# One inference step of a hybrid HGRN2 / RWKV-7 / short-conv layer: the RWKV stage laid out in 137 slots of TensorE's order

## The chip, the core and the metric

The kernel runs on one core of a Trainium2 chip. The metric is the device time of one execution in microseconds (us). The engines are named as in the profile: PE is TensorE's matmul, PEld its weight load, DVE VectorE, ACT ScalarE, POOL GpSimd, SP SyncE, which issues the DMAs. A kernel line is written L135.

## What is computed

One layer of a recurrent decoder takes 256 new tokens of one sequence and 8 tokens for each of 8 sampled sequences, 320 token columns in all. The layer's input is normalised and multiplied by one wide matrix; three branches (HGRN2, RWKV-7, a short convolution) work on its parts, are multiplied back to the model's width, gated and merged; an output matrix and a squared-ReLU MLP follow. The part that matters here is the RWKV branch:

```python
h = _rmsnorm(x, g_pre_mix)
proj = jnp.einsum('btd,de->bte', h, w_in)
rw = proj[..., OFF_RW:OFF_SC]
prev = jnp.concatenate([rw_prev[:, None], rw[:, :-1]], axis=1)
xs = rw + (prev - rw) * rw_mu
r, kr, vr, wd, ad, gd = jnp.split(xs, cuts, axis=-1)
w_log = -jax.nn.softplus(-(rw_w0 + jnp.tanh(wd) @ rw_w2)) - 0.5
decay = jnp.exp(-jnp.exp(w_log))
a = jax.nn.sigmoid(rw_a0 + ad @ rw_a2)
g = jax.nn.sigmoid(gd) @ rw_g2
kk = hs(kr * rw_k_k)
kk = kk / jnp.maximum(jnp.sqrt(jnp.sum(kk * kk, -1, keepdims=True)), 1e-12)
k = kr * (1.0 + (a - 1.0) * rw_k_a)
# per token and head:
#   S = S (diag(w) - kk^T (a*kk)) + v^T k ;  o = S r
o_rw, rw_S = _rwkv7_scan(r_, w_, k_, v_, kk, a_, rw_S0)
# group norm of o_rw per head, plus a bonus (sum of r*k*rw_r_k) * v, times g
y_b = o_rw @ w_pb
```

The model's width is 2048, the RWKV branch has 16 heads of width 64. The kernel evaluates the scan in chunks of 64 tokens, each with a triangular inverse.

## The kernel before

**Dense work.** Every large product is done in three matmuls of float32r halves, hi times ah, hi times al, lo times ah (L135 to L137 in `dense`), 128x320 each. `granule` loads 128x1024 weights (`raw`), and `split` makes `whi_t` on ScalarE (L109) and `wlo_t` on VectorE (L110), each in two pieces of 512. One output tile of the projection takes two granules, 16 k-steps and 48 matmuls. The order of the stages is: input norm and first tiles, RWKV stage (with the short convolution's tiles in it), HGRN with the merge of w_pc, the merges of w_pb and w_pa, output matrix, MLP.

**The RWKV stage** goes over 8 pairs of heads j (called heads here, j from 0), with two heads of 64 in the 128 partitions. For each there is
- `shift_mix`, three times: a projected tile (k, r, v) is taken out of PSUM into R (L305, L306), POOL makes the difference to the token before (L311), VectorE mixes (L314, L316).
- `rwkv_front`: the two small products for decay and a (L389), their activations (L395 to L397), the running product of decays Wp (L401), W (L403), its reciprocal Wi (L405); then the norm of kk: the square (L409), its sum over each head by a 128x320 matmul with a matrix of ones (L411), and one over its root in `rsqrt`, that is ScalarE's root (L170), VectorE's reciprocal (L171), two products on POOL and two VectorE passes (L174, L175); the normalised kk (L415) goes into LYR and BK, and transposes of v and BK follow (L440, L460). L451 sums r*k for the bonus.
- `rwkv_solve`: products of LYR and BK (L486), masked into Nb and GB (L495 to L500); the inverse of the 16x16 diagonal blocks on VectorE, 15 products and 15 sums (L517, L519) on a tile of 40 partitions that is reached through DRAM; then the inverse is widened to 32 and 64 with small matmuls (L542, L546, L552), whose results go back by L543, L549, L553.
- `rwkv_chunks`: for each of 4 chunks three steps, one behind the other: L586 with L587, copied to Y by ScalarE (L589); L594, copied to X by VectorE (L596); L598 with L599, which gives the next state (L604, L606). Then the sample part (L615 to L639) and the group norm (L649 to L668), whose matmul is L678, and at last L683.

What comes of it is B (L684), and the convolution's is Cb; both stay in SBUF until `merge_split` splits them for the merges.

**What sets the order.** The program is traced head by head; a list scheduler with simulated times then orders each engine's instructions by priority, the earlier traced first. Each engine runs its own list in order and waits on semaphores. On TensorE the small matmuls of a chain so come to stand between dense ones.

Of the kernel before, what the change touches and what calls it, by code (L numbers as in the profile page):

```python
# [88 lines left out]
SC_ORDER = ((), (0,), (1,), (2,), (3,), (4,), (5,), (6, 7))  # L89


class K:
# [31 lines left out]

    def dense(self, granules, ah, al):
# [53 lines left out]
    def build(self):  # L179
# [94 lines left out]
        self.merge_split(self.Cb)  # L274
# [5 lines left out]
        for src, i, w in ((self.B, 1, io["w_pb"]), (self.A, 0, io["w_pa"])):  # L280
            self.merge_split(src)
# [14 lines left out]
    def shift_mix(self, wp, n, name, packed):  # L296

        nc = self.nc
        ps = self.proj(n)
        i = n - RR  # L300
        R = wp.tile([128, 329], F32, name="R" + name, bufs=1)
        Rs = R[:, 257:329].rearrange("p (b w) -> p b w", w=9)
        nc.gpsimd.tensor_copy(R[:, 0:1], self.zero)
        nc.gpsimd.tensor_copy(Rs[:, :, 0], self.prev[:, i, :])
        nc.vector.tensor_mul(R[:, 1:257], ps[:, :NP], self.rs[:, :NP])  # L305
        nc.vector.tensor_mul(Rs[:, :, 1:9], ps[:, NP:].rearrange("p (b w) -> p b w", w=8),  # L306
                             self.rs[:, NP:].rearrange("p (b w) -> p b w", w=8))
# [12 lines left out]
    def rwkv(self, cx):  # L320
# [21 lines left out]
        for nm, cols in (("Nb", 640), ("GB0", 640), ("GB1", 640), ("LX", 256), ("Ms", 256), ("Od", 640)):  # L342
# [9 lines left out]
        for d in self.dP:  # L352
            nc.sync.dma_start(d[0:128 * 640].rearrange("(p x) -> p x", x=640), Z["Nb"])
        self.Z = Z
        xwa = self.shift_mix(w2, RWA, "k", True)
        self.L = kp.tile([128, NT], F32, name="L")
        nc.scalar.activation(self.L[0:64, :], xwa[0:64, :], AF.Tanh)
        nc.scalar.copy(self.L[64:128, :], xwa[64:128, :])
        self.Lg = kp.tile([128, NT], F32, name="Lg")
        st = [self.rwkv_front(0, wp, w2)]  # L360
        self.rwkv_solve(0, st[0], wp)
        xg = self.shift_mix(w2, RG, "v", True)
        nc.scalar.activation(self.Lg, xg, AF.Sigmoid)
        st.append(self.rwkv_front(1, wp, w2))
        for j in range(8):
            if j < 7:
                self.rwkv_solve(j + 1, st[j + 1], wp)
            self.rwkv_chunks(j, st[j], wp, w2)
            for i in SC_ORDER[j]:
                self.short_conv(i)  # L370
            if j < 6:
                st.append(self.rwkv_front(j + 2, wp, w2))
        nc.sync.dma_start(io["o_cv"], self.cvo)
        nc.sync.dma_start(io["o_shift"], self.shl)

    def rwkv_front(self, j, wp, w2):
# [25 lines left out]
        W = w2.tile([128, NT], F32, name="W")  # L402
        V.tensor_mul(W, Wp, wt[:, 1:])  # L403
        Wi = wp.tile([128, NT], F32, name="Wi")
        V.reciprocal(Wi, W)  # L405


        sq = wp.tile([128, NT], F32, name="sq")
        S.activation(sq, kx, AF.Square, scale=self.par("kk", j))  # L409
        ss = self.pa.tile([128, 512], F32, name="pa_t")  # L410
        T.matmul(ss[:, :NT], self.cst("bo1"), sq, start=True, stop=True)  # L411
        V.tensor_scalar_max(sq, ss[:, :NT], 1e-24)
        rn = self.rsqrt(wp, sq, "rn")
        kkn = rn
        V.scalar_tensor_tensor(kkn, kx, self.par("kk", j), rn, ALU.mult, ALU.mult)  # L415

        LYR = w2.tile([128, 5, 4, 64], F32, name="LYR")
        BK = w2.tile([128, 5, 3, 64], F32, name="BK")
# [12 lines left out]
        S.copy(BK[:, :, 2, :], BK[:, :, 0, :])  # L431
        rk = wp.tile([128, NT], F32, name="rkk")
        V.scalar_tensor_tensor(rk, r, self.par("rk", j), t, ALU.mult, ALU.mult)


        X = w2.tile([128, 5, 2, 64], F32, name="X")
# [12 lines left out]

        bs = self.pa.tile([128, 512], F32, name="pa_t")  # L450
# [12 lines left out]

        return W, LYR, BK, X, BT, vx

    def rwkv_solve(self, j, front, wp):
        nc, io = self.nc, self.io
        V, G, S, T = nc.vector, nc.gpsimd, nc.scalar, nc.tensor
        W, LYR, BK, X, BT, vx = front
# [5 lines left out]
        Nb = Z["Nb"].rearrange("p (c w) -> p c w", w=128)  # L475
        GB = Z["GB%d" % (j % 2)].rearrange("p (c h w) -> p c h w", h=2, w=64)
        for mk, cc in (("mkp", slice(0, 4)), ("mks", slice(4, 5))):
# [10 lines left out]
            for h, rows in ((0, lo), (1, hi)):  # L488
# [19 lines left out]
        nc.sync.dma_start(flat(dN), Z["Nb"])  # L508
        Nd = wp.tile([40, 16, 16], F32, name="Nd")
        Pd = wp.tile([40, 16, 16], F32, name="Pd")  # L510
        for c in range(5):
            nc.sync.dma_start(Nd[8 * c:8 * c + 8], blocks(dN, c))
        S.copy(Pd.rearrange("p s t -> p (s t)"), self.cst("eye16")[0:40])
        for u in range(15, 0, -1):
            w = 16 - u
            t1 = wp.tile([40, 16, 16], F32, name="t1")
            V.tensor_mul(t1[:, 0:u, 0:w], Nd[:, 0:u, u:u + 1].to_broadcast([40, u, w]),  # L517
                         Pd[:, u:u + 1, u:16].to_broadcast([40, u, w]))
            V.tensor_add(Pd[:, 0:u, u:16], Pd[:, 0:u, u:16], t1[:, 0:u, 0:w])  # L519
# [18 lines left out]
        for h in (16, 32):  # L538
            T3 = Z["T%d" % h].rearrange("p (c w) -> p c w", w=128)
# [687 lines left out]
```

## Time and profile before

| | |
|---|---|
| median of 3 runs | 2457.81 us (2457.61 to 2459.03) |
| the profiled execution | 2458.85 us |
| its span in the profile | 2457.0 us |
| mean granted TensorE clock | 0.993 |
| TensorE busy, whole span | 98% |
| VectorE, ScalarE, POOL busy | 61%, 41%, 15% |
| TensorE busy in the RWKV stage, 45 to 606 us | 540.57 of 561 us |
| HGRN with w_pc, 606 to 1000 us (start of it) | 394.00 of 394 us |

The page is of one execution on the chip. Busy time of matmuls is modelled at its end, as they are pipelined, so a busy TensorE need not be at its full pace; its pace is read from the number of matmuls in a stretch. The waits are the idle time of an engine and the instruction that ended it. The granted clock of TensorE is 1 where it runs at full speed.

### The profile page before, as it was taken

To read this page: it belongs to the slowest core of one execution; us is meant where nothing else is said; L and a number is where in the kernel's file an instruction comes from. 1 tells how busy PE (TensorE), PEld (TensorE's weight loads), DVE (VectorE), ACT (ScalarE), POOL (GpSimd) and SP (SyncE) were. 2 spreads that over 40 slices of the span, in tenths; PEclk is the share of its full clock that TensorE was granted. 3 is DMA by queue.
4 is the path that set the end of the run, shared out by engine and by line. 5 is a ranking of instruction groups with operands and counts; after the bars stand their busy time and mean duration, and the time that the engine had idled before them with its cause. 6 is when DMAs were issued, how large, how long until landed. Compare 5 with 4: busy or idle time off the path is not lost.

```text
span 2457.0 us, 41891 instructions
## 1 busy us (share of the span) xinstructions
PE 2413.6 (98%) x16134; PEld 2317.3 (94%) x16134; DVE 1508.5 (61%) x3209; ACT 1017.5 (41%) x2049; POOL 358.8 (15%) x508
## 2 busy tenths in 40 slices
PE   8999999999999999999999999999999999999998
PEld 7888898889999999999999897999999999999997
DVE  6788888876666666655555436654555555555555
ACT  6444444434444444433443335334333333333333
POOL 4323332221001100011111331200000000000003
PEclk9999999999999999999999999999999999999999
DMA  5423333334433443344444654444444444444443
GB/s 194 132 90 122 108 116 115 119 121 149 141 132 136 143 141 131 129 154 150 146 155 148 233 180 161 155 149 152 148 153 147 153 148 153 148 149 152 149 152 129
DMA packets 132278, 355.05 MB, mean 145 GB/s; under 512 B 34928, under 2 KB 43504, under 8 KB 132080
## 3 DMA queue, kind: packets, MB, share of 16 engines
q1 hardware_dynamic: 132080, 352.38, 41.8%
q8 instruction: 128, 2.10, 0.3%
q14 instruction: 70, 0.57, 0.1%
HBM read 337.19 MB, written 15.14 MB: 143 GB/s over the span
## 4 chain that ended last, share of the span: by engine, by line
PE 90%; DVE 7%; POOL 1%; ACT 1%; issue 1%; DMA 1%; SPq 0%; DVEq 0%; ACTq 0%; POOLq 0%
PE mm_t L135 26%; PE mm_t L137 26%; PE mm_t L136 26%; DVE wlo_t L110 1%; PE pi L486 1%; PE plv_t L851 1%; PE pho_t L901 1%; PE pi L546 1%; DVE t L517 0%; PE pi L552 0%; PE wide_t L972 0%; PE py_t L586 0%; PE wide_t L973 0%; DVE Wi L405 0%; DVE rn_y L171 0%
## 5 line engine op out<-in xcount | busy, mean ns | idle before, releaser
L109 ACT CAST whi_t<-raw 128x512 fp32r<-128x512 f32 x1192 | 687.3, 618 | 1103.0 <-PE mm_t L136 757.2
L110 DVE TENSOR_TENSOR wlo_t<-raw,whi_t 128x512 fp32r<-128x512 f32 x1192 | 829.1, 724 | 309.3 <-ACT whi_t L109 299.6
L135 PE MATMUL mm_t<-xh,whi_t 128*128 128x320 f32 x2048 | 645.2, 315 | 1.7 <-DVE Rk L306 1.2
L137 PE MATMUL mm_t<-xh,wlo_t 128*128 128x320 f32 x2048 | 641.2, 313 | 0.4 <-DVE wlo_t L110 0.4
L136 PE MATMUL mm_t<-xl,whi_t 128*128 128x320 f32 x2048 | 640.3, 313 | 0.0
L135 PEld LDWEIGHTS mm_t<-xh,whi_t 128*128 128x128 f32 x2048 | 386.2, 189 | 6.7 <-issue 1.8
L137 PEld LDWEIGHTS mm_t<-xh,wlo_t 128*128 128x128 f32 x2048 | 386.0, 189 | 3.0 <-issue 0.9
L136 PEld LDWEIGHTS mm_t<-xl,whi_t 128*128 128x128 f32 x2048 | 386.1, 189 | 1.6 <-issue 0.2
L135 PE MATMUL mm_t<-hh,whi_t 128*128 128x320 f32 x1232 | 381.6, 310 | 0.0
L136 PE MATMUL mm_t<-hl,whi_t 128*128 128x320 f32 x1232 | 380.9, 309 | 0.0
L137 PE MATMUL mm_t<-hh,wlo_t 128*128 128x320 f32 x1232 | 380.8, 309 | 0.0
L137 PE MATMUL mm_t<-rh,wlo_t 128*128 128x320 f32 x1024 | 316.4, 309 | 0.0
L135 PE MATMUL mm_t<-rh,whi_t 128*128 128x320 f32 x1024 | 316.4, 309 | 0.0
L136 PE MATMUL mm_t<-rl,whi_t 128*128 128x320 f32 x1024 | 316.4, 309 | 0.0
L135 PEld LDWEIGHTS mm_t<-hh,whi_t 128*128 128x128 f32 x1232 | 231.7, 188 | 6.5 <-ACT sqt L1058 4.9
L136 PEld LDWEIGHTS mm_t<-hl,whi_t 128*128 128x128 f32 x1232 | 231.6, 188 | 0.0
L137 PEld LDWEIGHTS mm_t<-hh,wlo_t 128*128 128x128 f32 x1232 | 231.6, 188 | 0.0
L136 PEld LDWEIGHTS mm_t<-rl,whi_t 128*128 128x128 f32 x1024 | 192.2, 188 | 0.0
L135 PEld LDWEIGHTS mm_t<-rh,whi_t 128*128 128x128 f32 x1024 | 192.2, 188 | 0.0
L137 PEld LDWEIGHTS mm_t<-rh,wlo_t 128*128 128x128 f32 x1024 | 192.2, 188 | 0.0
L1129 DVE TENSOR_TENSOR m<-m,mm_t 128x320 f32<-128x320 f32 x112 | 54.6, 488 | 189.4 <-PE mm_t L137 189.4
L1059 POOL TENSOR_TENSOR ssf<-ssf,sqt 128x320 f32<-128x320 f32 x14 | 14.1, 1004 | 841.9 <-issue 809.6
(425 smaller groups left out, 2744.4 us busy)
## 6 DMA issues: line engine op xcount, KB each, us to landing
raw<-w_in SPq DMA_DIRECT2D x256, 512.0 KB
raw<-w_ff SPq DMA_DIRECT2D x256, 512.0 KB
raw<-w_o SPq DMA_DIRECT2D x32, 512.0 KB
hs<-s_hg SPq DMA_DIRECT2D x16, 512.0 KB
raw<-w_pc SPq DMA_DIRECT2D x16, 512.0 KB
raw<-w_pb SPq DMA_DIRECT2D x16, 512.0 KB
raw<-w_pa SPq DMA_DIRECT2D x16, 512.0 KB
o_hgs<-hsn SPq DMA_DIRECT2D x16, 256.0 KB
```

What stands on the lines that cost most here:

```text
L109: self.nc.scalar.copy(hi, src)
L110: self.nc.vector.tensor_sub(lo, src, hi)
L135: mmul(ps[:, :NT], hi[:, w], ah[:, i, :], start=(i == 0), stop=False)
L136: mmul(ps[:, :NT], hi[:, w], al[:, i, :], start=False, stop=False)
L137: mmul(ps[:, :NT], lo[:, w], ah[:, i, :], start=False, stop=(i == n - 1))
L486: T.matmul(pp[h][:, i, :], BK[rows, c, h:h + 2, :].rearrange("p a w -> p (a w)"), LYR[rows, c, h:4:2, :], start=True, stop=True)
L546: T.matmul(ps[:, half(i)], Nb[:, i, :], cols(Mm[:, i, :], h, 0), start=True, stop=True)
L851: T.matmul(ps[:, 0:128], KM, rh[:, 0:2 * hb], start=True, stop=True)
L901: T.matmul(op[:, 256:320], s0[:, b, :], QX[:, 64 * b:64 * b + 64], start=(b == 0), stop=False)
L1059: (nc.vector if last else nc.gpsimd).tensor_add(acc, acc, t)
L1129: nc.vector.tensor_add(d, d, ps)
```

## The change

1. TensorE's order in the RWKV stage is laid by hand. Every part of a head (front, solve, chunk, sample, tail) becomes a generator that yields between its steps, and so do the dense tiles. A table gives each step of head j a slot, counted from 12(j+1); there are 137 slots, and 768 dense k-steps are spread over them: 7 a slot in the first 12, about 5.5 a slot after that. Only TensorE's order is fixed so; the other engines' lists still come from the scheduler, with a higher priority for the chunk, sample and late solve steps and a still higher one for the copies of projected tiles out of PSUM.
2. A granule is split in one piece of 1024, and up to three granules are fetched ahead.
3. The norm of kk: three 128x2 matmuls (L491 of the new kernel) sum the squares with the tokens in the partitions, six tiny VectorE operations on 128x6 (L495 to L501) and ScalarE's root (L496) make one over the root, ScalarE spreads it to 128x384 (L503), and three transposes (L507 to L509) bring it back.
4. The 16x16 inverse: 4x4 blocks first, then products of blocks of 4 and of 8, 18 VectorE operations in all.
5. `shift_mix` takes a tile out of PSUM in one operation and mixes in one.
6. More buffers (Nb 2, GB 3, LYR, X, BT 3, W 4, xsv 4; BK 1). B and Cb go to DRAM (dB, dC) and are loaded back by `merge_split`.

The core of the diff:

```diff
-SC_ORDER = ((), (0,), (1,), (2,), (3,), (4,), (5,), (6, 7))
+NSLOT = 12
+URGENT = 1000
+FRONT = (-6, -5, -3, 0, 1, 2)
+SOLVE = (0, 2, 9, 15, 16, 17, 18, 19, 20)
+SAMPLE = (20, 21, 22, 23)
+CONV = (3, 0, 1, 1, 1, 1, 1, 0)
+CHUNK = tuple(range(21, 33))
+TAIL = (33, 39, 40)
...
-        for q in range(2):
-            c = slice(512 * q, 512 * q + 512)
+        for q in range(pieces):
+            c = slice(1024 // pieces * q, 1024 // pieces * (q + 1))
             self.split(hi[:, c], lo[:, c], raw[:, c])
...
-    def dense(self, granules, ah, al):
+    def dense_steps(self, granules, ah, al):
...
                 i += 1
+                if i < n:
+                    yield
...
+    def fetch(self):
+        while len(self.ahead) < 3 and self.order:
+            n, h = self.order.pop(0)
+            with self.tc.high_priority(offset=URGENT):
+                self.ahead.append(self.granule(self.io["w_in"][n, h]))
+        return self.ahead.pop(0)
...
+        with self.tc.high_priority(offset=2 * URGENT):
+            nc.vector.tensor_mul(R[:, :, 1:9], g8(ps), g8(self.rs))
...
+        chains = ((front, FRONT), (sample, SAMPLE), (chunk, CHUNK), (solve, SOLVE), (tail, TAIL))
+        total = 8 * NSLOT + TAIL[-1] + 1
+        with self.tc.manual_schedule(engines={mybir.EngineType.PE}):
+            done = 0
+            for t in range(total):
+                for j in range(8):
+                    for chain, slots in chains:
+                        if t - NSLOT * (j + 1) in slots:
+                            if chain in (chunk, sample) or slots is SOLVE and t - NSLOT * (j + 1) > 9:
+                                with self.tc.high_priority(offset=URGENT):
+                                    next(chain[j], None)
+                            else:
+                                next(chain[j], None)
+                while done < max(7 * min(t + 1, NSLOT), blocks - (blocks - 7 * NSLOT) * (total - 1 - t) // (total - NSLOT)):
+                    next(dense, None)
+                    done += 1
...
-        T.matmul(ss[:, :NT], self.cst("bo1"), sq, start=True, stop=True)
-        V.tensor_scalar_max(sq, ss[:, :NT], 1e-24)
-        rn = self.rsqrt(wp, sq, "rn")
+        for i, c in enumerate((0, 128, 192)):
+            T.matmul(ss[:, 2 * i:2 * i + 2], sq[:, c:c + 128], self.cst("bo1")[:, 0:128:64], start=True, stop=True)
+        V.tensor_scalar_max(v6, ss[:, 0:6], 1e-24)
+        S.activation(t6, v6, AF.Sqrt)
+        V.reciprocal(y6, t6)
+        V.tensor_mul(t6, y6, y6)
+        V.tensor_mul(t6, t6, v6)
+        V.tensor_scalar(t6, t6, -0.5, 1.5, ALU.mult, ALU.add)
+        V.tensor_mul(y6, y6, t6)
+        S.copy(spread, y6.unsqueeze(2).to_broadcast([128, 6, 64]))
+        yield
+        T.transpose(rn[:, 0:128], full[:, 0, :], ident)
+        T.transpose(rn[:, 128:256], full[:, 1, :], ident)
+        T.transpose(rn[:, 256:320], full[64:128, 2, :], ident[64:128, 64:128])
...
-        for u in range(15, 0, -1):
+        for u in (3, 2, 1):
...
+        for n in (4, 8):
+            for o in range(0, 16, 2 * n):
+                a, b = slice(o, o + n), slice(o + n, o + 2 * n)
+                m = np_[:, 0:n * n].rearrange("p (s t) -> p s t", t=n)
+                product(m, Nd[:, a, b], Pd[:, b, b], n)
+                product(Pd[:, a, b], Pd[:, a, a], m, n)
...
+                t = wp.tile([128, NT], F32, name="bsrc")
+                self.nc.sync.dma_start(t, src[k])
+            self.split(self.bh[:, k, :], self.bl[:, k, :], t)
```

How rows of the program's order read: line, operation, out<-in with the names of the program and a running number, shape.

**First place: TensorE, the chunk chain of one head.** Before (L586 and L587, L594, L598 and L599 are the three steps):

```order
L586 MATMUL py_t_1912<-X_1160,LYR_1145 128x128
L587 MATMUL po_t_1893<-X_1160,LYR_1145 128x128
L137 MATMUL mm_t_2319<-xh_78,wlo_t_2323 128x320
L135 MATMUL mm_t_2319<-xh_78,whi_t_2322 128x320
L594 MATMUL py_t_1919<-Y_1894,Pm1_389 128x64
L136 MATMUL mm_t_2319<-xl_79,whi_t_2322 128x320
L137 MATMUL mm_t_2319<-xh_78,wlo_t_2323 128x320
L135 MATMUL mm_t_2319<-xh_78,whi_t_2322 128x320
L136 MATMUL mm_t_2319<-xl_79,whi_t_2322 128x320
L137 MATMUL mm_t_2319<-xh_78,wlo_t_2323 128x320
L598 MATMUL py_t_1923<-X_1160,BT_1177 128x128
L599 MATMUL po_t_1893<-X_1160,GB1_395 128x128
```

In the new order (there the steps are L714 and L715, L723, L728 and L729; L147 to L149 are dense), with 15 dense matmuls at the mark:

```order
L714 MATMUL py_t_3386<-X_1863,LYR_1753 128x128
L715 MATMUL po_t_2961<-X_1863,LYR_1753 128x128
L667 MATMUL pi_3393<-c_58,Pm1_400 128x128 x4
L466 MATMUL pa_t_3405<-L_430,lw_3399 128x320
L466 MATMUL pa_t_3408<-L_430,lw_3399 128x320
...
L723 MATMUL py_t_3451<-Y_2962,Pm0_399 128x64
L672 MATMUL pi_3455<-Mm_401,Nb1_404 128x64 x4
L491 MATMUL pa_t_3463<-c_58,sq_3461 128x2 x3
L147 MATMUL mm_t_3441<-xh_78,whi_t_3314 128x320
```

The steps of a chain stand 15 or 18 dense matmuls apart where they stood 2 to 5 apart, and those of different chains now stand together.

**Second place: the norm of kk on VectorE and ScalarE.** VectorE before, at the reciprocal of one head:

```order
L549 TENSOR_TENSOR T32_405<-pi_2664,c_58 128x8x32
L405 RECIPROCAL Wi_3276<-W_3274 128x320
L553 TENSOR_TENSOR Pm1_389<-Pm1_389,pi_2670 128x8x32
L171 RECIPROCAL rn_y_3283<-rn_t_3284 128x320
L428 TENSOR_TENSOR BK_3293<-tk_3298,Wi_3276 128x5x64
L596 COPY X_2520<-py_t_3476 64x64 x2
L110 TENSOR_TENSOR wlo_t_3671<-raw_3668,whi_t_3670 128x512
L174 TENSOR_SCALAR rn_t_3284<-rn_t_3284 128x320
L606 TENSOR_SCALAR X_2520<-py_t_3480,W_2487 64x64
L175 TENSOR_TENSOR rn_y_3283<-rn_y_3283,rn_t_3284 128x320
L606 TENSOR_SCALAR X_2520<-py_t_3480,W_2487 64x64
L415 SCALAR_TENSOR_TENSOR rn_y_3283<-xsk_3103,p_59,rn_y_3283 128x320
```

VectorE in the new order, head 5. Ahead of these rows stand L768 (a copy to Ms), L680, which adds L679's product to Pm, and L768 again:

```order
L482 RECIPROCAL Wi_3417<-W_3415 128x320
L121 TENSOR_TENSOR wlo_t_3531<-raw_3528,whi_t_3530 128x1024
L497 RECIPROCAL y6_3468<-t6_3469 128x6
L807 TENSOR_REDUCE gs_3548<-otm_2894 128x5
L498 TENSOR_TENSOR t6_3469<-y6_3468 128x6
L522 TENSOR_SCALAR tk_3593<-a_3403,p_59,omka_397 128x320
L499 TENSOR_TENSOR t6_3469<-t6_3469,v6_3467 128x6
L808 TENSOR_SCALAR gs_3548<-gs_3548 128x5
L523 TENSOR_TENSOR tk_3593<-tk_3593,xsk_3138 128x320
L500 TENSOR_SCALAR t6_3469<-t6_3469 128x6
L810 TENSOR_TENSOR otm_2894<-otm_2894,gs_3548 128x320
L501 TENSOR_TENSOR y6_3468<-y6_3468,t6_3469 128x6
```

ScalarE in the new order at the same head (L775 copies what L772 computes, L717 what L714 computes, L812 is the square for the group norm):

```order
L740 COPY otm_2894<-po_t_2961 64x256 x2
L759 COPY LX_412<-LYR_2976 64x2x8x8 x2
L775 COPY Y4_3509<-pa_t_3567 64x64 x2
L717 COPY Y_3573<-py_t_3575 64x64 x2
L617 COPY Pd_3819<-c_58 40x256
L812 ACTIVATE sq2_3552<-otm_2894 128x320
L503 COPY sq_3477<-y6_3468 128x384
L818 ACTIVATE gt_3557<-gv_3554 128x5
```

The 128x320 reciprocal of the norm is gone; the tiny operations that take its place are strung between the reciprocal of W (L482), a 1024-wide split (L121) and the group norm's and k's 128x320 operations, and the spread L503 stands behind the copies L717 and the square L812.

**Third place: TensorE where the spread is read, the same head.** At the mark stand 15 dense matmuls:

```order
L728 MATMUL py_t_3497<-X_1863,BT_1962 128x128
L729 MATMUL po_t_2961<-X_1863,GB2_410 128x128
L763 MATMUL pa_t_3512<-LX_412,s0_3506 128x64 x4
L679 MATMUL pi_3519<-Pm1_400,T32_420 128x64 x4
...
L772 MATMUL pa_t_3567<-X_2472,LYR_2354 128x128
L773 MATMUL pa_t_3567<-c_58,Ms_414 128x128
L714 MATMUL py_t_3575<-X_2472,LYR_2354 128x128
L715 MATMUL po_t_3572<-X_2472,LYR_2354 128x128
L507 MATMUL pa_t_3581<-c_58,sq_3477 128x128
L508 MATMUL pa_t_3581<-c_58,sq_3477 128x128
L509 MATMUL pa_t_3581<-c_58,sq_3477 128x64
```

Before, no matmul stood between the sum L411 and the normalised kk. Now L507 to L509 stand there, one slot behind L679.

More of the change, by code (lines that the diff above doesn't have):

```diff
@@ L138, in dense, with run @@
                 i += 1
+                if i < n:
+                    yield
         return ps[:, :NT]
+    @staticmethod
+    def run(steps):
+        while True:
+            try:
+                next(steps)
+            except StopIteration as e:
+                return e.value
+    def dense(self, granules, ah, al):
+        return self.run(self.dense_steps(granules, ah, al))
     def dense_wide(self, tiles, ah, al, psp, wpool):
@@ L361, in rwkv @@
[L361 to L372, printed above, removed]
+        self.st = [{} for _ in range(8)]
@@ new lines, in rwkv @@
+        dense = self.rwkv_dense(w2)
+        front = [self.rwkv_front(j, wp, w2) for j in range(8)]
+        solve = [self.rwkv_solve(j, wp) for j in range(8)]
+        chunk = [self.rwkv_chunks(j, wp, w2) for j in range(8)]
+        sample = [self.rwkv_sample(j, wp) for j in range(8)]
+        tail = [self.rwkv_tail(j, wp) for j in range(8)]
+        blocks = (50 - len(self.early)) * 16
+        chains = ((front, FRONT), (sample, SAMPLE), (chunk, CHUNK), (solve, SOLVE), (tail, TAIL))
+        total = 8 * NSLOT + TAIL[-1] + 1
@@ new lines, in rwkv @@
+        with self.tc.manual_schedule(engines={mybir.EngineType.PE}):
[12 more added lines that the diff above has]
+                    done += 1
+            self.run(dense)
+            for c in front + solve + chunk + sample + tail:
+                assert next(c, 0) == 0
@@ L373, in rwkv, with rwkv_dense @@
         nc.sync.dma_start(io["o_cv"], self.cvo)
         nc.sync.dma_start(io["o_shift"], self.shl)
+    def rwkv_dense(self, w2):
+        S = self.nc.scalar
+        tiles, conv = [], [(c, j) for j in range(8) for c in (SC, SH, SB)]
+        for j in range(8):
+            tiles += [(RK, j), (RR, j), (RV, j)] + ([(RG, 0)] if j == 1 else [])
+            for _ in range(CONV[j]):
+                tiles.append(conv.pop(0))
+        tiles = [(RWA, 0)] + tiles + conv
+        self.order = [(n + j, h) for n, j in tiles if n + j not in self.early for h in range(2)]
+        self.ahead = []
+        done = {}
+        for n, j in tiles:
+            if n in (SC, SH, SB):
+                c = done.setdefault(j, self.short_conv(j))
+                for end in c:
+                    yield
+                    if end:
+                        break
+                continue
+            name = {RK: "k", RR: "r", RV: "v", RWA: "k", RG: "k"}[n]
+            quick = n + j in self.early
+            xs = yield from self.shift_mix(w2, n + j, name)
+            if n == RWA:
+                S.activation(self.L[0:64, :], xs[0:64, :], AF.Tanh)
+                S.copy(self.L[64:128, :], xs[64:128, :])
+            elif n == RG:
+                S.activation(self.Lg, xs, AF.Sigmoid)
+            else:
+                self.st[j][name] = xs
+            if not quick:
+                yield
@@ L625, in rwkv_chunks @@
         both = self.cst("bi")
-        yp = self.py.tile([128, 512], F32, name="py_t")
+        yield
+        yp = self.pa.tile([128, 512], F32, name="pa_t")
         T.matmul(yp[:, 0:128], alpha(4), flat(X[:, 4]), start=True, stop=False)
```

235 lines of the change are left out of this document (149 added, 86 removed).

## The prediction

> **What bounds the kernel now.** I read the page's line of busy times first, then windows (start:end; busy time and instructions of PE, PEld, DVE, ACT, POOL; PEclk; DMA share; GB/s) over the RWKV stage and over the MLP:
>
> ```profile
> PE 2413.6 (98%) x16134; PEld 2317.3 (94%) x16134; DVE 1508.5 (61%) x3209; ACT 1017.5 (41%) x2049; POOL 358.8 (15%) x508
> 45.00:606.00 561.00, 540.57 (x3629) 492.11 (x3629) 452.32 (x1208) 250.51 (x535) 162.15 (x312) 0.99 0.36 116
> 1700.00:1800.00 100.00, 100.00 (x684) 100.00 (x683) 52.95 (x93) 36.94 (x67) 0.00 (x0) 1.00 0.44 153
> ```
>
> TensorE sets the time. The MLP row gives its pace on dense work: 100/684 = 0.146 us a matmul. The RWKV stage is the row where TensorE is not full; 20.4 us of its 561 are shown idle. The waits of TensorE from 25 to 606 (total, times, longest) name them:
>
> ```profile
> PE pa_t L678 <- DVE Od L668: 6.4, 7, 1.5
> PE pa_t L451 <- DVE rkk L433: 2.3, 4, 1.3
> PE pa_t L389 <- ACT L L357: 2.2, 1, 2.2
> PE pa_t L460 <- DVE BK L430: 1.6, 2, 1.2
> PE py_t L598 <- DVE X L596: 1.5, 5, 0.4
> PE mm_t L135 <- DVE Rk L306: 1.2, 1, 1.2
> PE pa_t L440 <- DVE Pd L519: 1.0, 1, 1.0
> PE pa_t L411 <- ACT sg L395: 0.8, 1, 0.8
> PE py_t L586 <- DVE X L604: 0.7, 4, 0.2
> ```
>
> These are 17.7 us, six shorter groups add 2.4. L389 and L411 (3.0) and about 0.9 of the small ones fall in the first tiles, before the slots can help. That leaves 16 us of visible waits that the change can take.
>
> More is hidden, since ends of matmuls are modelled. One step of the chunk chain, from the timeline (start, duration):
>
> ```profile
> 302.55 0.46 PE L586 MATMUL py_t<-X,LYR 128*128 128x128 f32 x2
> 302.99 0.39 PE L137 MATMUL mm_t<-xh,wlo_t 128*128 128x320 f32 x1
> 303.22 0.31 PE L135 MATMUL mm_t<-xh,whi_t 128*128 128x320 f32 x1
> 303.41 0.44 ACT L589 COPY Y<-py_t 64x64 f32<-64x64 f32 x2
> 303.89 0.43 PE L594 MATMUL py_t<-Y,Pm 128*128 128x64 f32 x2 [0.37 <-ACT Y L589]
> ```
>
> L135 starts at 303.22, and at the dense pace L594 could start at 303.37. It starts at 303.89, as ScalarE's copy ends at 303.85: 0.52 lost, 0.37 shown. At 0.15 for each of 96 such steps (8 heads, 4 chunks, 3 steps) that is 14 us at most, and none at least.
>
> **The change, part by part.** The sum is made against the profiled run's 2458.85 (span 2457.0), 1.0 above the median of the runs.
>
> *Old waits.* With 15 or 18 dense matmuls (2.2 to 2.6 us) between the steps of a chain, in place of 2 to 5, the 0.4 to 1.5 us of these rows are covered. The gain is 16 to 30. The returns to dense work become fewer, by my count 11 a head: the first dense matmul behind a group takes 0.39 where the next takes 0.31 (rows 302.99 and 303.22), so 11 x 8 x 0.08 = 7. Against this stand three 128x2 matmuls and three transposes for one L411 a head, which is 0 to 0.7 a head, 3 taken. I take 30 + 7 - 3 = 34, near the upper end, because every chain step that I followed got its whole 2.2 us. The ends are 16 and 45 (no L411 cost, and an early stretch at half clock gone too).
>
> *VectorE.* The norm of kk loses three 128x320 passes and a reciprocal, the inverse goes from 30 small operations to 18, and the split is one 1024-wide operation. VectorE has 452 us of work in 561, so nothing of this is on TensorE's path by itself: 0.
>
> *A new wait, at L507.* In the old order no matmul stands between the sum over kk and the normalised kk. Now there are three transposes, L507 to L509, and they read what ScalarE's L503 spreads out of y6, the last of six tiny VectorE operations (L497 to L501). VectorE runs its operations in the program's order. This is how a reciprocal there holds up what stands behind it:
>
> ```profile
> 281.45 0.36 DVE L553 TENSOR_TENSOR Pm<-Pm,pi 128x256 f32<-128x256 f32 x1
> 281.73 2.14 DVE L171 RECIPROCAL rn_y<-rn_t 128x320 f32<-128x320 f32 x1
> 283.79 0.43 DVE L428 TENSOR_TENSOR BK<-tk,Wi 128x320 f32<-128x320 f32 x1
> 284.13 0.45 DVE L596 COPY X<-py_t 64x64 f32<-64x64 f32 x2
> ```
>
> In the new order of head 5 (shown with the change) VectorE comes from L680, which needs TensorE's L679, and then has L768, the reciprocal L482, the split L121, the tiny operations, and between them L807, L522, L808, L523 and L810. So however early VectorE is, y6 follows L679 by at least the length of this piece. Durations by the nearest rows:
>
> ```profile
> L405 DVE RECIPROCAL Wi<-W 128x320 f32<-128x320 f32 x8 | 16.9, 2114 | 0.0
> L110 DVE TENSOR_TENSOR wlo_t<-raw,whi_t 128x512 fp32r<-128x512 f32 x204 | 137.9, 696 | 16.1 <-ACT whi_t L109 13.4 <-ACT Y L589 1.1 <-issue 0.2
> L1035 DVE TENSOR_TENSOR x<-x,m 128x640 f32<-128x640 f32 x8 | 6.4, 817 | 0.0
> L427 DVE TENSOR_TENSOR tk<-tk,xsk 128x320 f32<-128x320 f32 x8 | 4.9, 618 | 0.0
> L426 DVE TENSOR_SCALAR tk<-a,p,omka 128x320 f32<-128x320 f32 x8 | 3.5, 439 | 0.8 <-ACT a L396 0.7
> L649 DVE TENSOR_REDUCE gs<-otm 128x5 f32<-128x320 f32 x8 | 3.9, 483 | 0.4 <-ACT otm L639 0.3
> L624 DVE COPY Ms<-pa_t 64x128 f32<-64x128 f32 x16 | 4.6, 288 | 1.9 <-PE pa_t L619 1.6
> L650 DVE TENSOR_SCALAR gs<-gs 128x5 f32<-128x5 f32 x8 | 1.5, 189 | 0.0
> L654 ACT ACTIVATE sq<-otm 128x320 f32<-128x320 f32 x8 | 3.8, 470 | 3.4 <-DVE otm L652 3.4
> ```
>
> The 1024-wide split lies between one 512 (0.70) and two (1.39); from 0.70 at 512 and 0.82 at 640 the slope gives 1.18. Sum: L680 0.36 + L768 0.29 + 2.11 + 1.18 + L807 0.48 + L522 0.44 + L523 0.62 + L810 0.48 + six tiny ones at 0.17 (L650's 0.19 at most) = 7.0. Neighbours overlap by up to 0.08 (281.73 + 2.14 is 283.87, the next starts at 283.79) or not at all; 0.6 off for thirteen: 6.4. Then ScalarE: L812, the square of L810's result (0.47), stands ahead of L503 and starts with L501; L503 is 384 wide, by L654's rate 0.56. Together 0.9 behind y6, so L507 can start 7.3 us after L679. TensorE's way there is 15 dense matmuls (2.2) and two pairs, L772 with L773 and L714 with L715, at 0.44 (302.55 to 302.99): 3.1. **The wait is 4.2 us.** The same piece in heads 3, 4, 6 and 7 adds up to 8.0, 7.8, 6.0 and 7.5 (with a shift mix in it in 3 and 4, no split in 6), so waits of 5.8, 5.6, 3.8 and 5.3. Five heads: 25; 20 with the larger overlap and 18 dense matmuls everywhere, 28 with no overlap. The first three fronts run without this pin. Head 1's y6 stands among the first inverse's operations, 11 us of VectorE work against some 7 of TensorE; head 0's has 8 against 6.5: 8 in all (0 to 14).
>
> *The clock.* Long waits cost more than themselves here. Behind the two longest waits later in the program stand stretches at half clock:
>
> ```profile
> PE wide_t L699 <- POOL ue L698: 4.5, 1, 4.5
> PE nrm L1069 <- POOL ssb L1048: 2.6, 1, 2.6
> 110.07:606.00 495.93, 482.95 (x3287) 440.48 (x3286) 396.60 (x1080) 215.84 (x470) 134.64 (x258) 1.00 0.36 118
> 1390.07:1396.89 6.82, 5.42 (x13) 3.11 (x14) 3.71 (x5) 3.54 (x7) 3.46 (x3) 0.50 0.57 207
> 1536.84:1540.25 3.41, 1.45 (x10) 1.18 (x9) 3.41 (x3) 0.00 (x0) 3.25 (x3) 1.00 0.47 161
> 1540.25:1550.49 10.24, 9.61 (x41) 9.61 (x42) 2.90 (x11) 0.63 (x2) 0.58 (x1) 0.50 0.15 51
> ```
>
> From 110 to 606 no wait is over 1.5 us, and the granted clock is 1.00 throughout. The 2.6 us wait, and a stretch of 3.41 us in which TensorE was busy for 1.45, were enough for 10.24 us at 0.50; 4.5 us for 6.82 (three and two times 3.41). A wait of 3.8 to 5.8 us leaves less than that in one such stretch nearly wherever it falls. Some 5.5 us of the 6.8 lie behind the end of the wait, and half of that is lost at most: 2.5. Five heads: **12** (0 to 23).
>
> The Trainium skill, "TensorE: Matmul & The Clock Gate", Part 1, under "What's actually happening", says that the clock goes back to half after an idle window of some 3.4 us, and that the window runs freely. The row 1536.84:1540.25 differs: that window was busy for 1.45 us and the clock fell all the same, so by the trace a window need not be idle throughout.
>
> *The rest.* B and Cb now go through DRAM. Cb's loads come early; for B two loads are ahead and six wait for two buffers at the start of w_pb: 1 (0 to 5). SP's queue issues sixteen small stores more, with three granules loaded ahead of use: 0. From HGRN on the order is the old one: 0.
>
> Sum: 2458.85 - 34 + 25 + 8 + 12 + 1 = 2470.9, and **2470** on the median's scale, which the rivals use too.
>
> **Rivals.**
>
> 1. *The VectorE piece is not what L507 waits for* (faster). On ScalarE, L503 stands behind the copies L717 of what L714 and L715 have just computed, so TensorE waits at least about 0.2 + 0.44 (rows 302.55 to 303.41) + 0.47 + 0.56, or 1.7 us, at L507 whatever VectorE does. If that alone ends last, it is 5 x 1.7 = 8 without half clock: 2458.85 - 34 + 8 + 4 + 1 = 2437.9, or 2437 (4 for the first heads, with no half clock). It decides once the VectorE piece is under some 4 us. Against it: L482 and L121 alone take 3.3 of it. For it: each head sheds a 2.1 us reciprocal, and no row shows this piece itself, only its parts.
>
> 2. *The clock holds* for most of these waits: 2458.85 - 34 + 25 + 8 + 1 = 2458.9, or 2458. It is 2463 if the clock falls for two waits in five, which would be so if a stretch of 3.41 us had to be idle throughout: a wait of 4.9 us holds one whole in (4.9 - 3.41)/3.41 of the cases. Waits up to 1.5 us that leave the clock at 1.00 speak for a threshold; the 2.6 us row speaks against one so high. The Trainium skill's clock gate page, named above, would have it so.
>
> 3. *The slots do not remove the hidden part*, as each step's copies come late behind 1024-wide casts and splits: only 17 gained, and the new waits stay: 2458.85 - 16 + 25 + 8 + 12 + 1 = 2488.9, or 2488.
>
> **How the numbers follow.** About 0.2% (4.9 us) is what a measurement of this kernel can tell from no change, so the bounds are 2453 and 2463. The forecast has 0.47 (own range 2457 to 2482), rival 1 0.27, rival 2 0.16, rival 3 0.10. Faster: rival 1 and the low ends of the others, 0.32. Same: most of rival 2 and a part of the forecast, 0.19. Slower: 0.49. The range goes from just under rival 1 to just short of rival 3: 2433 to 2487.
>
> **What would show it.** In the waits, a line L507 <- ACT L503 with at least five times and 20 to 28 us, its longest near 5.8, right or wrong for the new wait; in the windows, PEclk under 0.98 for the stage, with stretches at 0.50 behind these waits, for the clock; no line left for L598, L451 and L678 above 0.5 in all, for the old waits. A total under 10 us at L507 makes the prediction wrong and gives rival 1. PEclk of 1.00 beside waits of 4 us gives rival 2; a chunk step that starts later than the dense pace allows, behind ScalarE or VectorE copies, gives rival 3.

## The result, and the profile after

The changed kernel takes 2478.06 us (median of 4 runs, 2475.27 to 2478.88) against 2457.71 us beside it: a ratio of 1.0083, 95% interval 1.0069 to 1.0098, so 20 us slower. The profiled execution has a span of 2475.8 us and a mean granted clock of 0.983.

The waits of TensorE in the RWKV stage, which now ends at 624 us (total, times, longest), and the windows of the same stretch as before:

```profile
PE pa_t L507 <- ACT sq L503: 52.6, 8, 9.1
PE pa_t L843 <- issue: 1.4, 1, 1.4
PE pa_t L784 <- DVE X L780: 1.0, 1, 1.0
PE pa_t L772 <- DVE Ms L768: 1.0, 1, 1.0
45.00:606.00 561.00, 504.01 (x3561) 484.67 (x3560) 425.21 (x943) 236.32 (x428) 148.75 (x300) 0.94 0.38 119
```

Of fifteen kinds of waits one of any size is left. It comes once a head, 6.6 us on average, and the clock of the stage fell from 0.99 to 0.94. The old waits are mostly gone: outside L507 there are 4.4 us of idle time where there were 20.4.

One of the eight waits, for head 5, in the timeline of VectorE, ScalarE and TensorE (start, duration, and in brackets the idle time before it and what ended it):

```profile
320.02 0.49 DVE L480 TENSOR_TENSOR W<-Wp,wt 128x320 f32<-128x320 f32 x1
320.55 0.28 DVE L768 COPY Ms<-pa_t 64x128 f32<-64x128 f32 x1
320.75 0.40 DVE L680 TENSOR_TENSOR Pm<-Pm,pi 128x256 f32<-128x256 f32 x1
...
321.50 2.15 DVE L482 RECIPROCAL Wi<-W 128x320 f32<-128x320 f32 x1
323.57 1.16 DVE L121 TENSOR_TENSOR wlo_t<-raw,whi_t 128x1024 fp32r<-128x1024 f32 x1
324.64 0.18 DVE L497 RECIPROCAL y<-t 128x6 f32<-128x6 f32 x1
...
326.08 0.82 DVE L500 TENSOR_SCALAR t<-t 128x6 f32<-128x6 f32 x1
326.82 0.48 DVE L810 TENSOR_TENSOR otm<-otm,gs 128x320 f32<-128x320 f32 x1
327.22 0.15 DVE L501 TENSOR_TENSOR y<-y,t 128x6 f32<-128x6 f32 x1
```

```profile
323.30 0.44 ACT L717 COPY Y<-py_t 64x64 f32<-64x64 f32 x2
327.65 0.40 ACT L617 COPY Pd<-c 40x256 f32<-40x256 f32 x1 [3.91 <-DMA dP<-Pd]
327.96 0.47 ACT L812 ACTIVATE sq<-otm 128x320 f32<-128x320 f32 x1
328.33 0.49 ACT L503 COPY sq<-y 128x384 f32<-128x384 f32 x1
```

```profile
322.87 0.39 PE L715 MATMUL po_t<-X,LYR 128*128 128x128 f32 x2
328.88 0.47 PE L507 MATMUL pa_t<-c,sq 128*128 128x128 f32 x1 [5.62 <-ACT sq L503]
```

The chain reads as the order had it: L680, the reciprocal, the split, the tiny operations between larger ones, the square, the spread, the transposes. VectorE is done with L501 at 327.37; ScalarE, held by L617 until 328.05, then delays the spread by some 0.6 us more. TensorE has nothing to do from 323.26 to 328.88. At the end of each of the eight waits a stretch at half clock begins (five of them as windows; the third number from the end is PEclk):

```profile
64.88:71.71 6.83, 5.41 (x20) 4.97 (x21) 3.78 (x11) 2.60 (x5) 0.39 (x2) 0.50 0.24 71
105.84:116.08 10.24, 3.62 (x13) 3.17 (x14) 7.96 (x15) 1.48 (x3) 3.62 (x6) 0.50 0.30 88
157.04:167.28 10.24, 4.68 (x17) 4.23 (x18) 8.11 (x16) 2.32 (x4) 0.68 (x1) 0.50 0.27 52
215.06:221.89 6.83, 5.72 (x21) 5.28 (x22) 4.82 (x16) 1.84 (x5) 0.00 (x0) 0.50 0.42 122
...
327.70:334.53 6.83, 5.65 (x21) 5.21 (x22) 5.45 (x17) 2.83 (x6) 0.00 (x0) 0.50 0.33 115
```

Where the time of the stage went can be added up from the starts of TensorE's records: for each two dense matmuls that follow each other, what lies between their starts beyond the dense pace of 0.1465 us, parted by whether small matmuls stand between them, after the shown idle time is taken out.

| us, from 45 to the first matmul of w_pc | before | after |
|---|---|---|
| length | 563.0 | 579.1 |
| idle time shown | 20.4 | 57.0 |
| groups of small matmuls (211, then 121 groups) | 158.5 | 138.8 |
| between dense neighbours, at full clock | 20.5 | 11.2 |
| between dense neighbours, at half clock | 3.4 | 15.7 |
| the dense matmuls themselves, at the pace | 358.9 | 356.6 |

The new wait costs 36.6 net of the old ones, the half clock 12.3; the groups of small matmuls give back 19.7 and the neighbours at full clock 9.3, or 29.0 together; 2.3 less lies in the dense matmuls of the stretch. These terms come to 17.6 where the length grew by 16.1. The start of the output matrix is 17.7 later, so 1.6 is lost between; 1.1 of it is shown as waits for the reloaded B at the start of w_pb. The end of the span is 18.8 later.

### The profile page after: what moved, and what is told of

It is laid out like the page before. It is cut to its first block, busy times and chain, and to the rows that moved or that the text cites. A ratio compares the mean times of both kernels' runs of the same rounds, so it can differ in the third digit from the quotient of the medians.

```text
span 2475.8 us, 40727 instructions
## 1 busy us (share of the span) xinstructions
PE 2394.9 (97%) x16190; PEld 2326.5 (94%) x16190; DVE 1447.6 (58%) x2485; ACT 961.5 (39%) x1467; POOL 357.9 (14%) x494
## 4 chain that ended last, share of the span: by engine, by line
PE 89%; DVE 5%; ACT 1%; DMA 1%; issue 1%; POOL 1%; SPq 0%; DVEq 0%; ACTq 0%; POOLq 0%
PE mm_t L147 27%; PE mm_t L148 27%; PE mm_t L149 27%; DVE wlo_t L121 1%; DVE t L633 1%; PE plv_t L1020 1%; PE pho_t L1070 1%; DMA dP<-Pd 1%; PE pi L587 0%; PE wide_t L1141 0%; ACT whi_t L120 0%; PE wide_t L1142 0%; PE wide_t L861 0%; DVE Wi L482 0%; DVE m L1328 0%
## 5 line engine op out<-in xcount | busy, mean ns | idle before, releaser
L120 ACT CAST whi_t<-raw 128x1024 fp32r<-128x1024 f32 (+1 forms) x600 | 625.6, 1044 | 1146.2 <-PE mm_t L148 997.0
L121 DVE TENSOR_TENSOR wlo_t<-raw,whi_t 128x1024 fp32r<-128x1024 f32 (+1 forms) x600 | 764.7, 1275 | 445.6 <-ACT whi_t L120 444.4
L147 PE MATMUL mm_t<-xh,whi_t 128*128 128x320 f32 x2048 | 654.1, 319 | 0.0
L149 PE MATMUL mm_t<-xh,wlo_t 128*128 128x320 f32 x2048 | 639.3, 312 | 0.0
L147 PEld LDWEIGHTS mm_t<-xh,whi_t 128*128 128x128 f32 x2048 | 390.7, 191 | 7.8 <-issue 3.5
L149 PEld LDWEIGHTS mm_t<-xh,wlo_t 128*128 128x128 f32 x2048 | 390.3, 191 | 0.0
L147 PE MATMUL mm_t<-hh,whi_t 128*128 128x320 f32 x1232 | 381.0, 309 | 0.0
L149 PE MATMUL mm_t<-hh,wlo_t 128*128 128x320 f32 x1232 | 380.2, 309 | 0.0
L149 PE MATMUL mm_t<-rh,wlo_t 128*128 128x320 f32 x1024 | 316.4, 309 | 0.0
L147 PE MATMUL mm_t<-rh,whi_t 128*128 128x320 f32 x1024 | 316.4, 309 | 0.0
L147 PEld LDWEIGHTS mm_t<-hh,whi_t 128*128 128x128 f32 x1232 | 231.3, 188 | 6.5 <-ACT whi_t L120 6.5
L149 PEld LDWEIGHTS mm_t<-hh,wlo_t 128*128 128x128 f32 x1232 | 231.2, 188 | 0.2 <-DVE wlo_t L121 0.2
L147 PEld LDWEIGHTS mm_t<-rh,whi_t 128*128 128x128 f32 x1024 | 192.2, 188 | 0.0
L149 PEld LDWEIGHTS mm_t<-rh,wlo_t 128*128 128x128 f32 x1024 | 192.2, 188 | 0.0
L1233 POOL TENSOR_TENSOR ssf<-ssf,sqt 128x320 f32<-128x320 f32 x14 | 19.6, 1397 | 834.8 <-ACT sqt L1232 834.8
```

The costliest lines, as they stand in the source:

```text
L120: self.nc.scalar.copy(hi, src)
L121: self.nc.vector.tensor_sub(lo, src, hi)
L147: mmul(ps[:, :NT], hi[:, w], ah[:, i, :], start=(i == 0), stop=False)
L149: mmul(ps[:, :NT], lo[:, w], ah[:, i, :], start=False, stop=(i == n - 1))
L1233: (nc.vector if last else nc.gpsimd).tensor_add(acc, acc, t)
```

## The experiments

All ratios are to the kernel before, run beside each.

**1. e1_urgent: the norm's chain ahead in VectorE's and ScalarE's lists.**

```diff
-        V.tensor_scalar_max(v6, ss[:, 0:6], 1e-24)
...
-        S.copy(spread, y6.unsqueeze(2).to_broadcast([128, 6, 64]))
+        with self.tc.high_priority(offset=URGENT):
+            V.tensor_scalar_max(v6, ss[:, 0:6], 1e-24)
...
+            S.copy(spread, y6.unsqueeze(2).to_broadcast([128, 6, 64]))
```

> The changed kernel with one edit: the six tiny VectorE operations of the norm, ScalarE's root and the spread are traced with the higher priority of the chunk steps, so in VectorE's order they stand ahead of the split L121 and in five heads ahead of the reciprocal of W; TensorE's order is the same. Theory A (the wait at the transposes, 52.6 us in 8 times, with some 19 us lost at half clock behind it, is what the change pays): by the new order the wait falls to 8 to 16 us in all, at most two stretches at half clock are left, and the time is 2478 - 40 - 15 = about 2423 (2412 to 2435). Theory B (the wait is only where VectorE's general lateness shows, and the next TensorE step that needs VectorE waits as long): waits move to other lines, and the time stays above 2468.

Measured: 2441.38 us, ratio 0.994 (0.9925 to 0.9955). It beats both kernels: the kernel before by 14 us, the changed one by 37 by the two medians, or by 34 when each is taken against the kernel before that ran beside it (2457.71 and 2455.07). The waits (the added line moves the numbers up by one):

```profile
PE pa_t L508 <- ACT sq L504: 10.9, 3, 5.3
PE pi L588 <- DVE BK L525: 3.1, 2, 2.1
PE pi L588 <- DVE gt L821: 2.7, 1, 2.7
PE py_t L729 <- DVE X L726: 2.4, 3, 1.6
PE pi L588 <- DVE gt L822: 2.1, 1, 2.1
PE pi L588 <- DVE BK L527: 2.1, 1, 2.1
```

TensorE's order is the same; so it was what stands in VectorE's and ScalarE's lists ahead of the spread that cost these 34 to 37 us. Both lists were changed at once, so this run does not part them. The wait at the transposes fell from 52.6 to 10.9. But the time missed its range by 6 us: 10 us are now waited at the solve's first step L588, and five stretches at half clock are left where at most two were expected. Theory A holds for the larger part and theory B for a rest.

**2. oldnorm: the old norm in the new slots**, with no TensorE step inside its chain.

```diff
-        for i, c in enumerate((0, 128, 192)):
-            T.matmul(ss[:, 2 * i:2 * i + 2], sq[:, c:c + 128], self.cst("bo1")[:, 0:128:64], start=True, stop=True)
...
+        T.matmul(ss[:, :NT], self.cst("bo1"), sq[:, :NT], start=True, stop=True)
+        V.tensor_scalar_max(sq[:, :NT], ss[:, :NT], 1e-24)
+        kkn = self.rsqrt(wp, sq[:, :NT], "rn")
```

> The changed kernel with the norm of kk as it was before (one 128x320 matmul of ones, 128x320 root, reciprocal and passes), so that no TensorE instruction stands inside the norm's chain; slots, inverse, splits and copies stay new. Theory A: no line of that place in the waits, no half clock from it, 2478 - 52.6 - 19 + about 5 for the longer VectorE passes = about 2412 (2405 to 2428), far below the kernel before. Theory B: VectorE has eight more 2.1 us reciprocals and three more passes a head to carry, its lateness grows, 2470 or more.

Measured: 2475.05 us, 1.0075 (1.0059 to 1.0092): theory A missed clearly, and theory B's 2470 or more holds. The waits have moved to the solve's first step, here L570:

```profile
PE pi L570 <- DVE BK L509: 19.9, 4, 8.3
PE pi L570 <- DVE gr L806: 8.7, 2, 5.2
PE pa_t L522 <- DVE xsv L353: 6.8, 1, 6.8
PE pi L570 <- DVE gt L804: 6.3, 1, 6.3
```

L570 needs LYR and BK, the front's end, in its fixed slot. It is waited for 40.3 us. So taking the transposes out does not take the wait out: the front is late without them too, and TensorE meets it one step later. VectorE has more to do here (441 us busy in 45:606, 425 in the changed kernel), so this run does not tell its amount of work from the order of its list.

**3. warm: useless matmuls ahead of the transposes**, to part the price of the clock from that of the wait.

```diff
+        for _ in range(11):
+            T.matmul(rn[:, :NT], self.cst("bo1"), self.cst("m01"), start=True, stop=True)
         T.transpose(rn[:, 0:128], full[:, 0, :], ident)
```

> The changed kernel with eleven useless 128x320 matmuls of constants (about 0.41 us each, 4.5 us) ahead of the three transposes, into the tile that the transposes then overwrite. They fill most of each wait with TensorE work and leave VectorE's and ScalarE's orders as they are. If the half clock behind the waits costs what the rows say (8 stretches, 42 us of them behind the end of a wait, 45 percent lost, 19 us): PEclk 1.00 in the stage, and 2478 - 19 = about 2459 (2454 to 2466), though TensorE does 36 us more work. If the clock costs little: 2478 or more (to 2485), whatever PEclk shows.

Measured: 2461.70 us, 1.0025 (1.0014 to 1.0035). TensorE does 88 matmuls more and the kernel is 16 us faster than without them, by the two medians, or 14 when each is taken against the kernel before beside it. The windows row of the stage, and the wait that is left:

```profile
45.00:606.00 561.00, 549.52 (x3834) 515.86 (x3832) 434.24 (x968) 241.76 (x440) 151.96 (x301) 1.00 0.41 123
PE pa_t L509 <- ACT sq L503: 6.3, 3, 3.2
```

The granted clock of the stage is 1.00; one stretch of 3.41 us at half clock is left of eight. The orders of VectorE and ScalarE are all but the same (some 20 of VectorE's 2485 rows moved). Eleven of the matmuls take 6.1 us in the trace, not the 4.5 that were expected, so that in most heads they fill the whole wait: from TensorE's last step to the transposes it is 53.8 us in all, where it was 52.6. So these 14 to 16 us are the price of the half clock, and the waiting itself stayed as long as it was.

**4. slots_only: old norm, old inverse, splits of 512, no priority for the copies out of PSUM.** The diff is that of oldnorm with these parts put back as in the kernel before.

> The changed kernel with the old norm, the old inverse of 30 VectorE operations, splits in two pieces of 512 and no priority for the copies out of PSUM: the slots, the buffers and the way of B and Cb through DRAM are what is left of the change. Theory A: the slots alone bring most of what the change gains: 2420 to 2440. Theory B: VectorE, with all its old work and a fixed TensorE order, is late everywhere: 2460 or more.

Measured: 2465.40 us, 1.0038 (1.0023 to 1.0053): theory B; slower than the kernel before, and faster than the whole change. Of its 48.8 us of idle time in 45:606 most is again at L570 (27.9 us). So the loss is there with the slots, the buffers and the way through DRAM alone; these three were not parted. Against oldnorm, putting the inverse, the splits and the copies' priority back gains 10 us, though experiments 9 to 11 find no gain from any one of them put back in e1_urgent; why was not tried.

**5. u2: priority also for the block behind the transposes.** The same `with` around the lines from `rn` to BK.

> The kernel e1_urgent with the same priority also for the block behind the transposes (normalised kk, LYR, BK), up to the product for the bonus. In e1_urgent 10 us were waited at L588, the first solve step, for what this block makes. If the order of VectorE's list is what counts (theory A, widened: each TensorE step of the front waits for what stands ahead of its operands on VectorE), these waits go and the time falls by 10 and some half clock, to about 2429 (2422 to 2436). If VectorE has simply too much work in this stretch (theory B), the wait moves to another step and the time stays within 2436 to 2446.

Measured: 2440.40 us, 0.9937 (0.9922 to 0.9951): theory B. The waits at L588 went, and as much is waited elsewhere:

```profile
PE pa_t L786 <- DVE X L782: 9.4, 7, 2.2
PE pa_t L509 <- ACT sq L504: 9.3, 3, 5.2
PE pi L669 <- DMA Pm<-dP: 2.5, 1, 2.5
```

The idle time of 45:606 is 28.1 us against 28.0 in e1_urgent. VectorE is busy for four fifths of the stage, but ahead of these waits it has no room. One stretch of 20 us that ends where a wait at L786 ends (the third pair of numbers is VectorE):

```profile
239.56:259.56 20.00, 17.77 (x134) 17.35 (x132) 19.56 (x41) 10.87 (x21) 8.13 (x16) 1.00 0.44 122
```

**6. f765u: the front's first steps one slot earlier.**

```diff
-FRONT = (-6, -5, -3, 0, 1, 2)
+FRONT = (-7, -6, -3, 0, 1, 2)
```

> The kernel u2 with the first two steps of the front one slot earlier (slots -7, -6, -3 in place of -6, -5, -3), so that the norm's chain has a slot of TensorE work more, 2.4 us of dense and the small steps of one slot. Theory A: the waits at L508 and L588 fall to under 8 us in all, no half clock but at the first two heads, 2415 (2407 to 2425). Theory B: no change against u2, within 4 us.

Measured: 2442.43 us, 0.9949 (0.9931 to 0.9968); 27.5 us idle. Theory B again: against u2 the waits at L509 and L786 fall by 5.7 us and those at L563 and L730 grow by 5.4.

**7. oldnorm764: the old norm with the front one slot earlier.** `FRONT = (-7, -6, -4, 0, 1, 2)` in oldnorm.

> The kernel oldnorm (no transposes; 46 us were waited at L570, the first solve step, and ten stretches stood at half clock) with the front's first three steps one slot earlier (-7, -6, -4). If the wait is a matter of the slots given to the chain: each of the eight waits of 5 us shrinks by about a slot, 4 us, and the half clock mostly goes: about 2430 (2420 to 2442). If VectorE's amount of work is the limit: above 2462.

Measured: 2458.39 us, 1.0011 (1.0002 to 1.002), between the two theories. One slot more takes 17 us off, so the slots given to the chain count; 24 us are still waited at L570 (40.3 in oldnorm, not the 46 that were put), and eight stretches at half clock are left in the stage of oldnorm's nine.

**8. bef_norm: the new norm alone in the kernel before.** The norm's lines of the diff, and nothing else; TensorE's order is the scheduler's.

> The kernel before with one edit, the new norm of kk (three 128x2 matmuls, tiny operations, spread, three transposes), its TensorE order left to the scheduler. If it is the fixed slot of the transposes that costs, the scheduler puts them where their operand is ready: waits at them under 6 us in all, 2452 (2446 to 2460). If the transposes are late in any order, being behind a chain over three engines: 2470 or more.

Measured: 2460.07 us, 1.0013 (1.0004 to 1.0023), just above the end of the first theory's range. Its condition holds: the transposes (here L427) were waited for once, 2.0 us:

```profile
PE pa_t L694 <- DVE Od L684: 6.5, 7, 1.2
PE py_t L614 <- DVE X L612: 4.2, 7, 1.0
PE pa_t L389 <- ACT L L357: 2.2, 1, 2.2
PE pa_t L427 <- ACT sq L424: 2.0, 1, 2.0
```

So the new norm is waited for only where TensorE's order is fixed. VectorE is busy 433 us in 45:606 where it was 452, and that brings nothing there.

**9. e4_urgent_oldinv: the old inverse in e1_urgent.**

> The kernel e1_urgent (2441) with the old inverse of the 16x16 blocks, 30 small VectorE operations. In the traces the old inverse takes 51.6 us of VectorE in the stage (L517 26.8, L519 24.8), the new one 52.6 (its eighteen operations have fewer but longer rows). If VectorE's time is what matters, no change: 2441 (2437 to 2446). If the number of steps of the chain matters, the old one comes late to the late solve steps: 2450 or more, with waits at the widening steps.

Measured: 2444.39 us, 0.9944 (0.9929 to 0.9959), not to be told from e1_urgent. The new inverse has fewer operations and takes no less time.

**10. e5_urgent_512: splits in two pieces in e1_urgent.**

> The kernel e1_urgent with each split in two pieces of 512 again. VectorE pays 1.39 us a granule in place of 1.30, ScalarE 1.24 in place of 1.04: about 9 and 19 us more work over the stage, but no single operation of 1.2 us stands ahead of a small one. Theory: VectorE's amount of work counts, so it gets slower by a few us, 2445 (2440 to 2452). Rival: the length of one operation ahead of a tiny one counts, then faster, 2432 to 2438.

Measured: 2445.83 us, 0.9958 (0.9941 to 0.9974): some 4 us more, as for the amount of work, though the intervals overlap.

**11. e6_urgent_noevac: no priority for the copies out of PSUM in e1_urgent.**

> The kernel e1_urgent without the priority for the copies of projected tiles out of PSUM. If these copies' place counts, dense matmuls wait for their PSUM tile and shift mixes come later: 2448 or more with L147 among the waits. If not: 2441 within 4 us.

Measured: 2440.79 us, 0.9934 (0.992 to 0.9949): no difference. Taken out of e1_urgent one at a time, this priority and the new inverse change nothing that can be measured.

**12. e7_nolo: VectorE's part of the split left out in the stage.**

```diff
+        if nolo:
+            self.nc.scalar.copy(hi, raw)
+            return hi, hi
         lo = (pool or self.wlo).tile([128, 1024], F32R, name="wlo_t")
```

> The kernel e1_urgent with the VectorE part of the split left out for the granules of the RWKV stage: the third matmul of each k-step reads hi in place of lo, so the low half of these weights is not computed. It takes some 95 operations of 1.3 us, about 120 us, off VectorE's 437 in the stage. If the 28 us that TensorE still waits in e1_urgent come from VectorE's amount of work, they fall to under 14, and the time to about 2420 (2412 to 2428). If they come from the length of chains over several engines: 2436 to 2442.

Measured: 2418.25 us, 0.9842 (0.9828 to 0.9857). The kernel leaves out the low half of these weights, so it does not compute the layer and only tells what the work costs. VectorE's busy time up to w_pc falls from 432 to 327 us, the idle time of TensorE in the stage from 28.0 to 12.5 us, and 10.0 of that are at the transposes of three fronts:

```profile
PE pa_t L511 <- ACT sq L507: 10.0, 3, 4.5
PE pa_t L777 <- DVE Ms L772: 1.6, 2, 1.0
```

So most of what e1_urgent still waits from head to head goes with VectorE's work; what is left stands mainly at the first fronts. An operation that is left out also stands ahead of nothing, so this run does not part amount from order by itself; that further changes of order alone (experiments 5 and 6) bring nothing speaks for the amount. Of the 23 us gained 15.5 are shown as idle time; where the rest lies was not worked out.

## Why the prediction was right, and where its terms were off

The forecast was 2470 with a range of 2433 to 2487, and the time is 2478. The mechanism it put first is the one found: TensorE at L507 behind VectorE's list, and half clock behind that. That the number came so near is in part luck: the wait at L507 is 52.6 us where 33 were put, the gain from old and hidden waits 45 where 34 were put, and these two misses offset. The sign set for the wait, 20 to 28 us with a longest near 5.8, was passed by far (52.6 and 9.1).

**Old waits, 16 us visible.** Right: 20.4 us idle before, 4.4 now outside L507.

**Hidden part and returns, 18 us** (14 + 7 - 3). Too small: 29.0, of which 19.7 in the groups and 9.3 between dense neighbours at full clock. There are 90 groups fewer, the 11 a head that were counted; how the 29 part into hidden waits and cheaper returns was not tried. The total gain of 45 is the upper end that was given.

**The wait in heads 3 to 7, 25 us.** The gaps are 6.0, 8.1, 5.6, 5.0 and 6.3 us where 5.8, 5.6, 4.2, 3.8 and 5.3 were worked out: 31 us. In head 5 the piece from L680 to y6 took 6.6 us where 6.4 were worked out, so the sum of rows held (L500 took 0.82 where 0.17 was put, and others were shorter). Two things at its ends were left out. VectorE was still at L480 when L679 was done at 320.12, so L680 began at 320.75. On ScalarE, L617 waited for the stores of the inverse until 327.65, and the square L812, whose operand was there at 327.30, began at 327.96.

**The first three fronts, 8 us.** This is the term that was mis-sized most: the gaps are 5.8, 9.1 and 6.6 us, 21.6 in all, above the 14 given as its end. For heads 0 and 1 it set 8 and 11 us of VectorE work against 6.5 and 7 of TensorE. In the trace y6 is done 10.1 and 13.5 us after L491, and TensorE's way from L491 to L507 is only 4.9 us in both. For head 2, VectorE reaches L495 late, 7.8 us after L491 is done:

```profile
146.40 0.78 PE L491 MATMUL pa_t<-c,sq 128*128 128x2 f32 x6
153.81 0.40 DVE L680 TENSOR_TENSOR Pm<-Pm,pi 128x256 f32<-128x256 f32 x1
154.99 0.17 DVE L495 TENSOR_SCALAR v<-pa_t 128x6 f32<-128x6 f32 x1
```

So "without this pin" does not hold there: L680 stands ahead of L495 in that head too.

**The clock, 12 us.** By starts, 12.3 us more are lost between dense matmuls at half clock, and experiment 3 gets back 14 to 16 by filling the waits. So the price is shown, not only read off. Its parts were other than put: eight stretches in the stage, where the kernel before had two, at 2.0 us each (15.7 in all), in place of five at 2.5. The Trainium skill, "TensorE: Matmul & The Clock Gate", Part 1, "What's actually happening", puts the window at 3413 ns, free-running; the stretches of 6.83 and 10.24 us agree with it. Its condition, a whole idle window, was met in each of the eight waits, so it would have given eight falls as well; in heads 1 and 2 the clock fell one window earlier than that, with TensorE busy for 0.90 and 1.42 us of the window before. It is e1_urgent that tells: its waits are shorter, none of them holds a whole window, and the clock fell five times all the same. A window before a fall in the changed kernel, head 2, and one in e1_urgent (the first pair of numbers is TensorE):

```profile
153.63:157.04 3.41, 1.42 (x10) 0.99 (x9) 3.33 (x15) 0.94 (x5) 2.30 (x6) 1.00 0.27 14
360.63:364.04 3.41, 1.29 (x18) 1.05 (x17) 3.41 (x10) 2.21 (x8) 1.11 (x1) 1.00 0.48 191
```

The five windows of e1_urgent were busy for 0.85 to 1.51 us. So the prediction read its row 1536.84:1540.25 rightly.

**Rivals.** That ScalarE's place alone decides (2437): against it, the copies L717 are done at 323.74 in the timeline above and VectorE's L501 only at 327.37; ScalarE adds 0.6 us behind it. That the clock holds: 0.94 in the stage. That the hidden part stays: the groups became cheaper by 19.7.

**What the prediction did not see** is that the transposes are not the only place that brings this wait. Experiment 2 has no transposes and loses 20 us all the same, at the next fixed step; experiment 8 has them without the slots, and they are hardly waited for. What costs is a TensorE order that is fixed in slots while VectorE's list is still made by simulated times and holds the front behind other work. In e1_urgent, where the list is mended, VectorE is busy for 432 of 543 us, and for 95 to 98% of the 20 us ahead of the longer waits at L786 that u2 has in its place. There, taking a wait away at one step (experiments 5 and 6) brings it back at another, and of what was tried only leaving out VectorE work (experiment 12) takes it out.

## What to carry to other kernels

When one engine's order is fixed by hand, read the other engines' lists at each step that it waits for: from the last operation that is pinned to it, add up all that stands ahead of the operand, needed or not, on every engine of the chain. A long idle time of TensorE costs more than its length, here 14 to 16 us of half clock on top of 53 us of waiting. Look at how busy the other engine is just ahead of a wait, not over the stage: where it is full there, moving operations within its list only moves the wait. e1_urgent, one priority, is the version to keep; u2 and experiments 6, 9 and 11 cannot be told from it.

## What the runs showed of the hardware that was not expected

The product of 8x8 blocks (8x8x8, 512 wide) is slow on VectorE for its size, and eats up what the fewer steps save:

```profile
L633 DVE TENSOR_TENSOR t<-Pd,np 40x512 f32<-40x512 f32 x8 | 9.3, 1168 | 0.1
L635 DVE TENSOR_REDUCE np<-t 40x64 f32<-40x512 f32 x8 | 5.4, 674 | 0.1
```

A 512-wide product with two broadcast operands takes 1.17 us on 40 partitions, where the 512-wide split of the kernel before took 0.70 on 128. The inverse is 52.6 us in the stage, and was 51.6.

The tiny L500 has a mean of 0.41 us where its neighbours L497 and L501 have 0.17 and 0.15. In the timeline above its 0.82 us lie beside a POOL product (L525, 325.69 to 326.87); whether that is the cause was not tried.
